# Second-half transposes six steps later, two gate blocks moved ahead of a projection, and mLSTM loads issued one chunk earlier

## The chip, the core and the metric

The kernel runs on one core of one Trainium2 chip. The metric is the device time in microseconds (us) of one execution. Engines are named as the profile names them: PE is TensorE (PEld its weight load), DVE is VectorE, ACT is ScalarE, POOL is GpSimd, and SP is the queue that issues all DMAs of this kernel.

## What is computed

A trunk of two layers for 1024 tokens of width 1024, in float32. Each layer adds a normed mixer and then a normed SwiGLU to the residual stream.

```
for layer in range(2):
    h = rmsnorm(x, pre_mix_g[layer])
    h = ab_mixer(h, ...) if layer == 0 else mlstm_mixer(h, ...)
    x = x + rmsnorm(h, post_mix_g[layer])
    h = swiglu(rmsnorm(x, pre_ffn_g[layer]), w_gate, w_up, w_down)   # width 2816
    x = x + rmsnorm(h, post_ffn_g[layer])

def mlstm_mixer(xn, ...):
    q, k, v, o, ig, fg = split(xn @ w_in + b_in)
    # per chunk of tokens, 8 heads: scores = (q k^T) * exp(decays); num = scores v + inter * (q C)
    # C = decay * C + (w k)^T v          (the state that passes from chunk to chunk)
    h = rmsnorm_per_head(num / max(|den|, exp(-m))) * head_g
    return (sigmoid(o) * h) @ w_out
```

## The kernel before, in words

The 1024 tokens are worked in two halves of 512 (a and b, or A and B in names), each held with features on the partitions. Every float32 operand of a large product is split into a rounded high part and the low rest ("hi", "lo"), and `mm3` makes a product of three matmuls (lines 125 to 127): hi·hi, hi·lo, lo·hi. The high part is a cast on ACT and the low part a subtraction on DVE: lines 106 and 107 for weights streamed by `W`, lines 130 and 131 (`split`) for everything else.

**Order.** The program is written as one main line of matmul blocks. Beside it run "side" generators (norms, transposes, mLSTM); each `yield` of a main block with cost c lets a side advance c times its pace steps. The framework's scheduler then settles the order on each engine, so the order that the engines really hold is shown below where it matters. Each engine works through its own order strictly, and so does the SP queue.

**Feedforward.** Each layer's SwiGLU is done on 2x2 blocks with seven products in place of eight (a Strassen-like scheme): operands are sums and differences of the two token halves and of weight blocks.
- `sandwich` adds the normed mixer output to the residual, norms the result (`xn`), and hands it to a `feature` function. For half B that is `feature_b`: it transposes xn on PE (line 376, into `pt`), evicts on ACT (line 378, `xb` and `xk`), then makes sums and differences on DVE (lines 381, 382, 383, 387) and the splits `s2` and `s3`. `feature_c` later splits `s1`, `a22` and `s4` (twelve operands).
- Meanwhile the main line runs `phase0(LATE)` (PE tile `p`) and `down_first` (PE tile `d`: eleven row blocks m0 to m10 of 12 matmuls, each with an operand from `prep2`: names `r20a`, `whid0a`, `wlod0a` in layer 0, `r21a`, `whid1a`, `wlod1a` in layer 1). When they are done, `down_first` copies its four results on ACT (line 593, `y`).
- Then `phase1` begins. `prep1` loads gate and up weights (`ri`, `rj`), makes four differences for each on POOL (lines 444 to 447: `t14`, `t23`) and splits them (`whit2..g`, `wlot2..g`, then `whit2..u`, `wlot2..u`). The first product `pa` for the gate needs `whit2..g`, the second, for the up weights, needs `whit2..u`.

**mLSTM.** `in1` is the input projection of a half: 24 steps for v and gates (`pv`), 8 blocks for q and k (`pimq`), 8 for the output gate o (`pimo`, sigmoid at line 929). `mlstm` runs a half in four chunks of 128 tokens: loads (`ab`, `iwb`, `qk`, `vt`, each from DRAM), transposes `pc` and `pk`, scores `sc` (line 1018), `pn` (lines 1034, 1036), state update `pu` and `cst` (lines 1045, 1048), the squares of h on ACT (line 1055), a power on POOL (line 1063), the scaling `nu` on DVE (line 1065), and the transposes `ph` (line 1075) that make `yT`. The projection (`popA`, `popB`) multiplies `yT` with `w_out`.

The first half's mLSTM runs beside the second half's `in1`; in the main line it is drained after q and k, and the eight o blocks come behind the projection `popA`, where they cover the norm work of `sandwich` "pA".

Of the kernel before, what the change touches and what calls it, by code (L numbers as in the profile page):

```python
# [8 lines left out]
F32 = mybir.dt.float32  # L9
# [5 lines left out]
P = 128  # L15
# [3 lines left out]
NT = 4  # L19
# [21 lines left out]
def trunk(ctx: ExitStack, tc: tile.TileContext, x, w_in, w_out, w_gate, w_up, w_down,  # L41
          m_in, m_v, m_g, m_out, lru_w, vecs, post_mix, post_ffn, v_bias, out):
    nc = tc.nc
# [10 lines left out]
    def unit(shape, dt=F32, name="u"):  # L54
        return up.tile(shape, dt, tag="u", name=name, bufs=NU)
# [7 lines left out]
    def ps_aux(shape, name):  # L63
        return pp.tile(shape, F32, tag="aux", name=name, bufs=4)
# [56 lines left out]
    W = Stream()  # L121
# [12 lines left out]
    def rstat(src, name, vector=False, junk=None):  # L134
        ss = sp.tile([P, 1], F32, tag="ss", name=f"ss{name}", bufs=4)
        if junk is None:
            junk = sp.tile([P, D], BF16, tag="junk", name=f"junk{name}", bufs=1)
        if vector:
            nc.vector.scalar_tensor_tensor(junk, src, 1.0, src, op0=OP.mult, op1=OP.mult,
                                           accum_out=ss)  # L140
        else:
            nc.scalar.activation(junk, src, AF.Square, accum_out=ss)
        v = sp.tile([P, 1], F32, tag="sv", name=f"sv{name}", bufs=4)
        nc.vector.tensor_scalar(v, ss, 1.0 / D, EPS, op0=OP.mult, op1=OP.add)
        r = sp.tile([P, 1], F32, tag="sr", name=f"sr{name}", bufs=4)
        nc.gpsimd.tensor_tensor(r, v, half[:, 0:1], op=OP.pow)
        return r

    def row(src, name):
        t = sp.tile([P, D + 16], F32, tag="row", name=name, bufs=1)  # L150
        n = src.shape[-1]
        nc.sync.dma_start(t[:, 0:n], src.partition_broadcast(P))
        return t[:, 0:n]

    def load_x(src, t, name):
        xt = unit([P, D], F32, name)
        nc.sync.dma_start(xt, src[t * P:(t + 1) * P])
        return xt

    def scaled(xt, name, vector=False):  # L160
        xn = unit([P, D], F32, f"xn{name}")
        r = rstat(xt, name, vector, xn)
        if vector:
            nc.vector.tensor_scalar(xn, xt, r, None, op0=OP.mult)
        else:
            nc.scalar.activation(xn, xt, AF.Copy, scale=r)
        return xn
# [33 lines left out]
    def sandwich(o, src, dst, g_row, h, g_next, feature, wait=0):  # L201

        name = o.name
        gr = row(g_row, f"gr{name}")
        xn = []
        for t in range(NT):
            while o.ready < t:
                yield
            y = o.y[t]
            rows = slice((h * NT + t) * P, (h * NT + t + 1) * P)  # L210
            xt = load_x(src, h * NT + t, f"xr{name}{t}")
            r = rstat(y, f"p{name}{t}", t % 2 == 1)
            nc.vector.tensor_tensor(y, y, gr, op=OP.mult)
            yield
            nc.vector.scalar_tensor_tensor(xt, y, r, xt, op0=OP.mult, op1=OP.add)
            nc.sync.dma_start(dst[rows], xt)
            yield
            xn.append(scaled(xt, f"n{name}{t}"))
            yield
        for _ in range(wait):  # L220
            yield
        yield from feature(xn, g_next, f"n{name}")
# [71 lines left out]
    class Project:  # L294
# [17 lines left out]
        def run(self, before_last=None):  # L312
            self.prep(0)
            for i, c in enumerate(self.chunks):
                last = i == len(self.chunks) - 1
                if last and before_last is not None:
                    before_last()
                self.prep(i)
                yield from accum_out(self.o, self.st, *c, i == 0, last, f"{self.o.name}{c[0]}")
# [549 lines left out]
    d_v = [dp.tile([NT, P, 8, 129], F32, tag=f"dv{h}", name=f"dv{h}") for h in range(2)]  # L869
    d_qk = [dp.tile([8, P, T], F32, tag=f"dqk{h}", name=f"dqk{h}") for h in range(2)]  # L870
# [63 lines left out]
    def mlstm(m):  # L934
        h = m.h
        while m.gates is None:
            yield
        gi, gf = m.gates
# [35 lines left out]
        nc.sync.dma_start(d_w[h], iw)  # L974
        yield
        m.yT = []
        for c in range(NT):
            cs = slice(c * P, (c + 1) * P)
            ab = unit([P, 8, P], F32, f"ab{h}{c}")
# [2 lines left out]
            dw = d_w[h].rearrange("(a s) j -> s a j", s=2)  # L982
            for s in range(2):
                nc.sync.dma_start(iwb[s * 64:(s + 1) * 64], dw[s, :, cs].partition_broadcast(64))
            qk = unit([P, 8, P], F32, f"qk{h}{c}")
            nc.sync.dma_start(qk, d_qk[h][:, :, cs].rearrange("a p j -> p a j"))
            vt = unit([P, 8, 129], F32, f"vt{h}{c}")
            nc.sync.dma_start(vt, d_v[h][c])
            pc = ps_aux([P, 40], f"pc{h}{c}")
            nc.tensor.transpose(pc, ce[:, cs], ident[0:40, 0:40])  # L990
            cem = sp.tile([P, 40], F32, tag="cem", name=f"cem{h}{c}", bufs=2)
# [49 lines left out]
            if not (h == 1 and c == NT - 1):  # L1041
                for i in range(4):
                    pu = ps_aux([P, 2, 129], f"pu{h}{c}{i}")
                    kwp = kw[:, 2 * i:2 * i + 2].rearrange("p a b -> p (a b)")
                    nc.tensor.matmul(pu, kwp, vt[:, 2 * i:2 * i + 2], start=True, stop=True)
                    for s in range(2):
                        rr = slice(s * 64, (s + 1) * 64)
                        nc.vector.scalar_tensor_tensor(cst[rr, i, s], cst[rr, i, s],
                                                       iwb[rr, i, P - 1:P], pu[rr, s],
                                                       op0=OP.mult, op1=OP.add)  # L1050
                    yield
            ss = sp.tile([P, 8], F32, tag="hss", name=f"hss{h}{c}", bufs=2)
            for hd in range(8):
                junk = sp.tile([P, P], BF16, tag="junkh", name=f"jh{h}{c}{hd}", bufs=1)
# [52 lines left out]
    src_ffn(0, LATE)  # L1107
    src_in1()
    src_in1()
    o_part = W.src[-8:]  # L1110
    del W.src[-8:]
    src_proj(m_out, OUT1)
    W.src += o_part
    src_ffn(1, EARLY)
# [3 lines left out]
    x1 = dp.tile([S, D], F32, tag="x1", name="x1")  # L1118
    x2 = dp.tile([S, D], F32, tag="x2", name="x2")
    x3 = dp.tile([S, D], F32, tag="x3", name="x3")  # L1120
# [3 lines left out]
    def start(gen, pace):  # L1124
        s = [gen, pace, 0.0]
        sides.append(s)
        return s
# [15 lines left out]
    def drain(s):  # L1143
        if s in sides:
            sides.remove(s)
            for _ in s[0]:
                pass
# [10 lines left out]
    def gf(l):  # L1158
        return lambda k: ("g_ffn", 8 * l + k)
# [11 lines left out]
    f0, f1 = Ffn(0), Ffn(1)  # L1171
# [5 lines left out]
    gb = in0(mb, xb)  # L1177
# [8 lines left out]
    run(f0.phase0(EARLY))  # L1186
    drain(sb)
    ob = Out("oB")
    gb = start(sandwich(ob, x, x1, post_mix[0:1], 1, gf(0), f0.feature_b), 1.0)
    run(Project(mb.yT, ob, OUT0).run())  # L1190
    run(f0.phase0(LATE))
    run(f0.down_first())
# [6 lines left out]
    gb = start(sandwich(fb, x1, x2, post_ffn[0:1], 1, gm(1), into(xmb), 8), 1.0)  # L1199
# [4 lines left out]
    gb = in1(nb, xmb)  # L1204
    run(gb, 32)
    drain(sa)
    pa = Out("pA")
    ga = start(sandwich(pa, x2, x3, post_mix[1:2], 0, gf(1), f1.feature_a), 1.2)
    run(Project(na.yT, pa, OUT1).run())
# [3 lines left out]
    run(f1.phase0(EARLY))  # L1213
    drain(sb)
    pb = Out("pB")
    gb = start(sandwich(pb, x2, x3, post_mix[1:2], 1, gf(1), f1.feature_b), 1.0)
    run(Project(nb.yT, pb, OUT1).run())
    run(f1.phase0(LATE))
    run(f1.down_first())
# [5 lines left out]
    gb = start(sandwich_last(eb, x3, out, gr, 1), 1.0)  # L1225
# [91 lines left out]
```

## Time and profile before

| what | value |
|---|---|
| median of 3 runs | 2169.37 us (2169.26 to 2172.45) |
| profiled execution, its own time | 2169.25 us |
| span of the profiled execution | 2167.4 us |
| mean granted PE clock | 0.979 of full speed |
| busy: PE, PEld | 2064.0 us (95%), 1678.2 us (77%) |
| busy: DVE, ACT, POOL | 1494.2 us (69%), 931.7 us (43%), 506.9 us (23%) |

The span is the time from the first to the last instruction; 1.85 us of the execution lie around it. PE is busy nearly all the time, so what a change can save or cost is in the short stretches in which PE waits, and in those in which its clock is granted at half speed. All times in rows are counted from the start of the span.

### The profile page before, as it was taken

The page shows a single profiled execution, that of the slowest core. Times are in us where ns is not written, and L with a number is a line of the kernel's source. Part 1 is how long each engine was busy: PE and PEld are TensorE (multiplying, and loading weights), DVE is VectorE, ACT ScalarE, POOL GpSimd, SP SyncE. Part 2 cuts the span into 40 slices and gives each one's busy share as a digit, 9 for nine tenths or more (in the row PEclk, how much of TensorE's full clock was granted, in tenths as well). Part 3 has the DMA queues.
Part 4 walks back from the last instruction along what each step waited for, and adds up shares of the span by engine and source line. Part 5 has one row for each costly group of instructions (what it writes and reads, how often), then busy time and mean ns, then how long its engine had stood idle before and what let it go on. Part 6 is the DMA issues. An engine that isn't in the chain of part 4 may idle for free.

```text
span 2167.4 us, 26100 instructions
## 1 busy us (share of the span) xinstructions
PE 2064.0 (95%) x9200; PEld 1678.2 (77%) x9200; DVE 1494.2 (69%) x2103; ACT 931.7 (43%) x1317; POOL 506.9 (23%) x371
## 2 busy tenths in 40 slices
PE   7998989988999999999999998999988999999998
PEld 6776766766888887787988987778877888888786
DVE  6988689868876676558553764546459877766567
ACT  6754586446222222446253333645545222223453
POOL 2000100013743336501010000100015744436310
PEclk9999999998999999999999999999998999999999
DMA  6232544446544459967473852667455644469966
GB/s 230 88 122 68 190 141 146 136 160 229 165 160 162 162 182 328 380 201 255 131 257 104 243 178 88 230 188 216 153 177 193 218 162 157 158 211 364 329 223 218
DMA packets 202740, 417.39 MB, mean 193 GB/s; under 512 B 19920, under 2 KB 48720, under 8 KB 202608
## 3 DMA queue, kind: packets, MB, share of 16 engines
q1 hardware_dynamic: 202608, 415.72, 56.9%
q8 instruction: 72, 1.18, 0.2%
q14 instruction: 60, 0.49, 0.1%
HBM read 302.82 MB, written 112.82 MB: 192 GB/s over the span
## 4 chain that ended last, share of the span: by engine, by line
PE 45%; issue 4%; DVE 2%; DMA 2%; ACT 1%; POOL 0%; SPq 0%; DVEq 0%; POOLq 0%; ACTq 0%
PE d L126 4%; PE d L127 3%; PE d L125 3%; PE pb L125 2%; PE pb L126 2%; PE pb L127 2%; PE pc L127 2%; PE pc L126 2%; PE pc L125 2%; PE p L127 2%; PE p L125 2%; PE p L126 2%; PE pv L127 1%; PE pv L125 1%; PE pv L126 1%
## 5 line engine op out<-in xcount | busy, mean ns | idle before, releaser
L107 DVE TENSOR_TENSOR wlo<-raw,whi 128x1024 fp32r<-128x1024 f32 (+2 forms) x164 | 191.5, 1169 | 156.0 <-ACT whi L106 144.9
L106 ACT CAST whi<-raw 128x1024 fp32r<-128x1024 f32 (+2 forms) x164 | 164.6, 1007 | 276.8 <-PE p L126 56.4
L746 DVE SCALAR_TENSOR_TENSOR acc<-cy,vec,acc 128x512 f32<-128x512 f32 x240 | 168.8, 743 | 0.2
L131 DVE TENSOR_TENSOR wlod1s<-r21s,whid1s 128x1024 fp32r<-128x1024 f32 x44 | 56.3, 1286 | 47.7 <-ACT whid1s L130 46.9
L131 DVE TENSOR_TENSOR wlod0s<-r20s,whid0s 128x1024 fp32r<-128x1024 f32 x44 | 57.7, 1314 | 42.2 <-ACT whid0s L130 39.9
L125 PE MATMUL p<-xTnoA,whi 128*128 128x512 f32 x176 | 72.8, 416 | 12.9 <-ACT gel L721 9.1
L130 ACT CAST whid1s<-r21s 128x1024 fp32r<-128x1024 f32 x44 | 46.4, 1054 | 65.2 <-PE d L127 49.4
L130 ACT CAST whid0s<-r20s 128x1024 fp32r<-128x1024 f32 x44 | 46.4, 1054 | 60.5 <-PE d L127 55.5
L126 PE MATMUL p<-xTnoA,whi 128*128 128x512 f32 x176 | 71.9, 408 | 0.0
L1063 POOL TENSOR_TENSOR hrr<-hss,half 128x8 f32<-128x8 f32 x8 | 13.1, 1641 | 251.0 <-DVE hss L1061 251.0
L125 PE MATMUL p<-xTnpA,whi 128*128 128x512 f32 x176 | 71.4, 409 | 0.0
L127 PE MATMUL p<-xTnpA,wlo 128*128 128x512 f32 x176 | 71.1, 404 | 0.0
L126 PE MATMUL p<-xTnpA,whi 128*128 128x512 f32 x176 | 71.0, 403 | 0.0
L126 PE MATMUL d<-wlod0s,whid0s 128*128 128x512 f32 x176 | 69.3, 394 | 1.7 <-DVE wlod0s L131 1.7
L127 PE MATMUL p<-xTnoA,wlo 128*128 128x512 f32 x176 | 70.5, 405 | 0.0
L126 PE MATMUL d<-wlod1s,whid1s 128*128 128x512 f32 x176 | 69.5, 395 | 0.0
L127 PE MATMUL d<-whid1s,wlod1s 128*128 128x512 f32 x176 | 69.4, 394 | 0.0
L127 PE MATMUL d<-whid0s,wlod0s 128*128 128x512 f32 x176 | 68.6, 390 | 0.0
L125 PE MATMUL d<-whid1s 128*128 128x512 f32 x176 | 63.6, 397 | 3.4 <-DVE yeA L611 3.4
L131 DVE TENSOR_TENSOR wlod0a<-r20a,whid0a 128x1024 fp32r<-128x1024 f32 x33 | 44.8, 1363 | 29.4 <-ACT whid0a L130 25.9
L490 DVE TENSOR_TENSOR u<-pc,u 128x512 f32<-128x512 f32 x44 | 30.2, 690 | 44.7 <-PE pc L127 44.7
L540 POOL TENSOR_TENSOR wt<-wq 128x512 f32<-128x512 f32 x22 | 37.2, 1690 | 92.4 <-DMA wq<-in_w_down 52.0
(2481 smaller groups left out, 6561.0 us busy)
## 6 DMA issues: line engine op xcount, KB each, us to landing
wq<-in_w_down SPq DMA_DIRECT2D x88, 256.0 KB, 5.1
ft<-wt SPq DMA_DIRECT2D x88, 256.0 KB, 5.2
raw<-in_w_in SPq DMA_DIRECT2D x32, 512.0 KB, 3.6
raw<-in_m_in SPq DMA_DIRECT2D x32, 512.0 KB, 4.3
raw<-in_w_gate SPq DMA_DIRECT2D x22, 512.0 KB, 4.3
raw<-in_w_up SPq DMA_DIRECT2D x22, 512.0 KB, 3.6
fp<-p1f SPq DMA_DIRECT2D x44, 256.0 KB, 2.1
fs<-s SPq DMA_DIRECT2D x44, 256.0 KB, 3.7
```

The source lines that it names most:

```text
L106: nc.scalar.copy(hi[:, 0:n], raw[:, 0:n])
L107: nc.vector.tensor_tensor(lo[:, 0:n], raw[:, 0:n], hi[:, 0:n].bitcast(F32), op=OP.subtract)
L125: nc.tensor.matmul(ps, l[0], r[0], start=first, stop=False, **kw)
L126: nc.tensor.matmul(ps, l[0], r[1], start=False, stop=False, **kw)
L127: nc.tensor.matmul(ps, l[1], r[0], start=False, stop=last, **kw)
L130: nc.scalar.copy(dst_hi, src)
L131: nc.vector.tensor_tensor(dst_lo, src, dst_hi.bitcast(F32), op=OP.subtract)
L490: TT(u3[k], c[k], u3[k], op=OP.add)
L540: sub(t[0][:, 0], q[0][:, 1], q[0][:, 0], op=OP.subtract)
L746: nc.vector.scalar_tensor_tensor(dst, src[:, k:k + T], V(wname, w0 + k), dst, op0=OP.mult, op1=OP.add)
L1063: nc.gpsimd.tensor_tensor(rr, ss, half, op=OP.pow)
```

## The change

Four edits. Both `sandwich` calls that end in `feature_b` get `wait=6`: six empty steps between the last norm and the first transposition. Two of the eight o blocks of half B are run between the drain of the first mLSTM and the projection `popA`; the weight stream is put in that order. In `mlstm`, `qk` and `vt` of a chunk are issued by a function `load`: those of chunk 0 before the chunk loop, those of chunk c+1 after chunk c's state update.

```diff
+        def load(c):
+            qk = unit([P, 8, P], F32, f"qk{h}{c}")
+            nc.sync.dma_start(qk, d_qk[h][:, :, c * P:(c + 1) * P].rearrange("a p j -> p a j"))
+            vt = unit([P, 8, 129], F32, f"vt{h}{c}")
+            nc.sync.dma_start(vt, d_v[h][c])
+            return qk, vt
+
+        loaded = load(0)
         for c in range(NT):
...
-            qk = unit([P, 8, P], F32, f"qk{h}{c}")
-            nc.sync.dma_start(qk, d_qk[h][:, :, cs].rearrange("a p j -> p a j"))
-            vt = unit([P, 8, 129], F32, f"vt{h}{c}")
-            nc.sync.dma_start(vt, d_v[h][c])
+            qk, vt = loaded
...
+            if c + 1 < NT:
+                loaded = load(c + 1)
             ss = sp.tile([P, 8], F32, tag="hss", name=f"hss{h}{c}", bufs=2)
...
-    o_part = W.src[-8:]
-    del W.src[-8:]
+    o_part = W.src[-6:]
+    del W.src[-6:]
     src_proj(m_out, OUT1)
     W.src += o_part
...
-    gb = start(sandwich(ob, x, x1, post_mix[0:1], 1, gf(0), f0.feature_b), 1.0)
+    gb = start(sandwich(ob, x, x1, post_mix[0:1], 1, gf(0), f0.feature_b, 6), 1.0)
...
     run(gb, 32)
     drain(sa)
+    run(gb, 2)
     pa = Out("pA")
...
-    gb = start(sandwich(pb, x2, x3, post_mix[1:2], 1, gf(1), f1.feature_b), 1.0)
+    gb = start(sandwich(pb, x2, x3, post_mix[1:2], 1, gf(1), f1.feature_b, 6), 1.0)
```

What the scheduler makes of it is seen in the orders. The first place is on PE, layer 0, where `feature_b`'s transposes stand among `down_first`'s matmuls. `xnnoB_3477`, `_3511`, `_3545` and `_3593` are the four normed token tiles in turn; `whid0a_3736` is the first row block's operand. Before:

```order
L127 MATMUL d_3729<-whid0a_3736,wlod0a_3737 128x512
L126 MATMUL d_3730<-wlod0a_3737,whid0a_3736 128x512
L127 MATMUL d_3730<-whid0a_3736,wlod0a_3737 128x512
L376 MATMUL ptnoB_3605<-ident,xnnoB_3545 128x128
L376 MATMUL ptnoB_3612<-ident,xnnoB_3545 128x128
L376 MATMUL ptnoB_3649<-ident,xnnoB_3545 128x128
L376 MATMUL ptnoB_3656<-ident,xnnoB_3545 128x128
L376 MATMUL ptnoB_3605<-ident,xnnoB_3593 128x128
```

The same place on PE in the changed kernel, where `whid0a_3680` and `whid0a_3727` are the first two row blocks' operands:

```order
L125 MATMUL d_3675<-whid0a_3727 128x512
L125 MATMUL d_3676<-whid0a_3680 128x512
L126 MATMUL d_3676<-wlod0a_3681,whid0a_3680 128x512
L127 MATMUL d_3676<-whid0a_3680,wlod0a_3681 128x512
L125 MATMUL d_3676<-whid0a_3727 128x512
L376 MATMUL ptnoB_3635<-ident,xnnoB_3545 128x128
L376 MATMUL ptnoB_3642<-ident,xnnoB_3545 128x128
L376 MATMUL ptnoB_3700<-ident,xnnoB_3545 128x128
L376 MATMUL ptnoB_3707<-ident,xnnoB_3545 128x128
L126 MATMUL d_3673<-wlod0a_3728,whid0a_3727 128x512
```

Before, the third tile's transposes followed 6 `d` matmuls and the fourth's came directly behind them, ahead of the last 12 `p` matmuls. Now those 12 and 16 `d` matmuls stand ahead of the third tile's, and 40 `d` matmuls in all ahead of the fourth's.

The second place is on DVE, layer 1, at the start of `feature_b`'s sums. Before:

```order
L215 SCALAR_TENSOR_TENSOR xrpB_12755<-ypB_12408,srppB_12762,xrpB_12755 128x1024
L144 TENSOR_SCALAR svnpB_12786<-ssnpB_12784 128x1
L381 TENSOR_TENSOR xsnpB_12824<-xbnpB_12792,xknpB_12791 128x512
L382 TENSOR_TENSOR xbnpB_12792<-xanpB_12793,xbnpB_12792 128x512
L383 TENSOR_TENSOR xanpB_12793<-xsnpB_12824,xanpB_12793 128x512
```

And the same place on DVE in the changed kernel:

```order
L215 SCALAR_TENSOR_TENSOR xrpB_12755<-ypB_12408,srppB_12762,xrpB_12755 128x1024
L144 TENSOR_SCALAR svnpB_12786<-ssnpB_12784 128x1
L131 TENSOR_TENSOR wlod1a_13031<-r21a_13027,whid1a_13030 128x1024
L131 TENSOR_TENSOR wlod1a_13050<-r21a_13046,whid1a_13049 128x1024
L131 TENSOR_TENSOR wlod1a_13069<-r21a_13065,whid1a_13068 128x1024
L131 TENSOR_TENSOR wlod1a_13088<-r21a_13084,whid1a_13087 128x1024
L381 TENSOR_TENSOR xsnpB_12852<-xbnpB_12822,xknpB_12821 128x512
```

Four low halves of row blocks m4 to m7 have come ahead of the first sum (m3's and the product at line 423 too, a few rows further up); in layer 0 it is those of m1 to m4 and that product.

The third place is on PE at the end of the first mLSTM, with its last state updates `pu`, the transposes `ph` and the projection `popA`. Before:

```order
L1036 MATMUL pn_10290<-vt_10196,pr_10267 128x129 x2
L1045 MATMUL pu_10296<-vt_10196,kw_10255 128x258
L1045 MATMUL pu_10300<-vt_10196,kw_10255 128x258
L1045 MATMUL pu_10304<-vt_10196,kw_10255 128x258
L1045 MATMUL pu_10308<-vt_10196,kw_10255 128x258
L1075 MATMUL ph_10339<-ident,nu_10270 128x128 x4
L1075 MATMUL ph_10348<-ident,nu_10270 128x128 x4
L125 MATMUL popA_10385<-whi_10137,yspA_10357 128x512
```

The same place on PE in the changed kernel:

```order
L125 MATMUL pimo_10397<-xTnfB_8402,whi_10209 128x512
L126 MATMUL pimo_10397<-xTnfB_8402,whi_10209 128x512
L127 MATMUL pimo_10397<-xTnfB_8402,wlo_10210 128x512
L1083 MATMUL ph_10339<-ident,nu_10270 128x128 x4
L1083 MATMUL ph_10348<-ident,nu_10270 128x128 x4
L125 MATMUL popA_10453<-whi_10359,yspA_10425 128x512
```

The 48 matmuls of two o blocks now stand between the scores and `ph`: 17 of them among the `pn`, 17 between the last `pn` and the last `pu`, and 14 directly ahead of `ph`.

## Rows read from the trace of the kernel before

**Rows 1.** PE's waits, grouped: engine, line, waited for; us in total, times, longest.

```profile
PE ph L1075 <- DVE nu L1065: 6.0, 1, 6.0
...
PE pa L125 <- ACT whit210u L130: 5.2, 1, 5.2
PE pa L125 <- ACT whit200u L130: 5.1, 1, 5.1
PE ptnpB L376 <- ACT xnnpB L166: 4.8, 2, 2.9
PE ptnoB L376 <- ACT xnnoB L166: 4.4, 2, 2.7
...
PE pk L996 <- DMA qk<-dqk: 2.9, 2, 1.9
```

**Rows 2.** Stretches: busy us (instructions) of PE, PEld, DVE, ACT, POOL; granted clock; DMA.

```profile
484.20:494.40 10.20, 5.61 (x20) 3.91 (x19) 3.64 (x8) 6.26 (x9) 1.61 (x3) 0.51 0.72 255
492.66:542.30 49.64, 42.71 (x176) 33.94 (x175) 44.98 (x52) 29.96 (x45) 18.15 (x10) 0.91 0.70 228
1617.50:1627.70 10.20, 6.80 (x21) 5.23 (x22) 4.72 (x8) 6.73 (x12) 0.55 (x1) 0.51 0.75 255
1624.17:1671.04 46.87, 40.82 (x164) 32.28 (x163) 45.98 (x51) 30.28 (x46) 18.67 (x10) 0.86 0.66 219
1306.90:1313.70 6.80, 3.69 (x12) 3.03 (x13) 4.04 (x11) 2.18 (x4) 1.46 (x1) 0.51 0.00 1
```

**Rows 3.** PE in order of time, layer 0: start, us, instruction, [idle before].

```profile
470.39 0.40 PE L125 MATMUL p<-xTnoA,whi 128*128 128x512 f32 x1
470.63 0.39 PE L126 MATMUL p<-xTnoA,whi 128*128 128x512 f32 x1
...
480.25 0.73 PE L125 MATMUL d<-whid0a 128*128 128x512 f32 x2 [0.47 <-ACT whid0a L130]
483.52 0.50 PE L126 MATMUL d<-wlod0a,whid0a 128*128 128x512 f32 x1 [2.53 <-DVE wlod0a L131]
...
490.36 2.37 PE L376 MATMUL ptnoB<-ident,xnnoB 128*128 128x128 f32 x8 [2.72 <-ACT xnnoB L166]
```

**Rows 4.** DVE in order of time, the same columns, both layers' second halves.

```profile
492.66 0.69 DVE L381 TENSOR_TENSOR xsnoB<-xbnoB,xknoB 128x512 f32<-128x512 f32 x1 [4.16 <-ACT xknoB L378]
...
541.09 1.21 DVE L131 TENSOR_TENSOR wlot200u<-t2300u,whit200u 128x1024 fp32r<-128x1024 f32 x1
...
1647.40 1.78 DVE L383 TENSOR_TENSOR xanpB<-xsnpB,xanpB 128x512 f32<-128x512 f32 x1
```

**Rows 5.** POOL and ACT in order of time, layer 0 ahead of the first `pa`.

```profile
519.09 1.30 POOL L444 TENSOR_TENSOR t1400g<-rj00g,ri00g 128x512 f32<-128x512 f32 x1 [29.96 <-DMA rj00g<-in_w_gate]
...
526.89 0.58 ACT L593 COPY y<-d 128x512 f32<-128x512 f32 x1
```

**Rows 6.** DVE groups of 492.66 to 518.50 by form: count, busy us, mean ns, idle before.

```profile
L131 DVE TENSOR_TENSOR wlod0a<-r20a,whid0a 128x1024 fp32r<-128x1024 f32 x8 | 9.8, 1220 | 0.2 <-ACT whid0a L130 0.2
```

**Rows 7.** PE in order of time, layer 1's second half.

```profile
1601.30 0.39 PE L125 MATMUL p<-xTnpA,whi 128*128 128x512 f32 x1
...
1621.88 2.37 PE L376 MATMUL ptnpB<-ident,xnnpB 128*128 128x128 f32 x8 [2.94 <-ACT xnnpB L166]
```

**Rows 8.** PE, DVE and ACT in order of time, from the end of the first mLSTM on.

```profile
1298.15 1.14 PE L1034 MATMUL pn<-cst,qi 128*128 128x258 f32 x4
...
1301.84 1.91 PE L1045 MATMUL pu<-vt,kw 128*128 128x258 f32 x8
1309.77 1.94 PE L1075 MATMUL ph<-ident,nu 128*128 128x128 f32 x8 [6.02 <-DVE nu L1065]
...
1312.97 2.49 DVE L131 TENSOR_TENSOR yspA<-myT,yspA 128x512 fp32r<-128x512 f32 x4
...
1422.37 1.28 ACT L421 ACT_TABLE_LOAD   x1
```

**Rows 9.** DVE in order of time, the first mLSTM's first chunk.

```profile
1200.06 2.19 DVE L999 SCALAR_TENSOR_TENSOR ab<-ab,cem,mask 128x128 f32<-128x128 f32 x8 [4.84 <-DMA ab<-da]
```

## The prediction

> **What bounds the kernel.** I read the page's busy shares first: PE is busy in 95% of the span, so elsewhere than in PE's waits and its half-clock stretches nothing can be gained. Then the grouped waits of PE [rows 1]. The edits aim at three of their kinds: the transposes of half B that wait for the normed tiles (4.4 and 4.8 us), the one wait of 6.0 us at the end of the first mLSTM, and two waits of 2.9 us together for q and k loads. Then the stretches [rows 2], to see what the clock adds: behind each cluster of waits PE runs at 0.51 of full speed, that is mostly at the 1.2 GHz level. It is busy for 5.61 us of such a stretch in layer 0, 6.80 us in layer 1, 3.69 us at the mLSTM's end. Half of that busy time is what the lower level costs: 2.8, 3.4 and 1.8 us. The Trainium skill ("TensorE: Matmul & The Clock Gate", section Terms) prices such time at its length times one minus the granted share, which would be 5.1, 5.1 and 3.4 us; the rows show PE idle for much of it, so I keep the smaller prices.
>
> **Term 1, layer 0's transposes.** At stake are the waits at `ptnoB` of 4.4 us [rows 1], the wait of 2.53 us for the first low half [rows 3] and 2.8 us of clock: 9.7 us. The new order puts 12 `p` and 40 `d` matmuls ahead of the fourth tile's transposes. From 480.25 less 0.47 us, at 0.23 us from start to start [rows 3], those 52 end at 491.8, with the transposes between at about 492.4; the fourth tile was there by 490.36, so those waits go.
>
> What is late next is VectorE. Its first sum of `feature_b` began at 492.66, and from there to the end of `wlot200u`, 542.30 [rows 4], it was busy for 44.98 of 49.64 us [rows 2]. PE's second `pa` product needs that operand. Now the sums begin some 2 us behind those transposes (the evictions of line 378 lie between), at 494.5: 1.8 us later than before. What has moved ahead of them are four low halves of 1.22 us [rows 6] and one product like the sums, 0.69 [rows 4], 5.6 us. So `wlot200u` ends at 542.3 + 1.8 - 5.6 = 538.5, 3.8 us earlier, or up to 4.7 us earlier still if VectorE's idle time (49.64 - 44.98) closes. Against this stands GpSimd: beside its subtractions a VectorE sum takes 1.78 us [rows 4] where it takes 0.69 otherwise (1647.40 against 492.66). `prep1`'s loads follow the low halves through the five `raw` buffers, so the subtractions come earlier too, and into the sums. And ScalarE now has the four copies of line 593, 0.58 us each [rows 5], and the last casts of `s2` and `s3`, shaped alike, ahead of `whit200g`: some 3.4 us, which start only as `d` ends. I take 3 us of gain, bounds +1 (the ScalarE chain decides) to -8.5.
>
> A page states why this can eat the whole gain: by the Trainium skill ("SBUF — State Buffer", section "Who interferes with whom") a VectorE instruction with two SBUF inputs and a GpSimd instruction that reads SBUF exclude each other for a whole instruction. The trace agrees: 0.69 and 1.30 us [rows 4, 5] one after the other are near the 1.78 measured. By that rule eight subtractions of 1.30 us cost VectorE 10.4 us wherever they fall among its sums, and only VectorE's idle time can hide them.
>
> **Term 2, layer 1's transposes.** The same edit, but at stake are 4.8 us of waits and 3.4 of clock. PE now passes 48 `p` and 52 `d` matmuls from 1601.30 before the fourth tile's transposes: 23 us, and with the other transposes about 1626, where they stood at 1621.88 [rows 7]. VectorE's first sum moves from 1624.17 to 1628.2, 4.0 us later; five low halves and the product, 6.8 us, move ahead of it. From there to 1671.04, the end of `wlot210u`, VectorE was busy for 45.98 of 46.87 us [rows 2]: no slack here. So `wlot210u` ends 2.8 us earlier by VectorE's work. But the row blocks m4 to m7 are split early, so the weight loads and GpSimd's subtractions come earlier against the sums, `d` ends long before `whit210g` can be made, and PE's idle time lies in one piece in front of `pa` in place of several. ScalarE reaches `whit210u` only behind `whit210g`, two casts of b22 and twelve of `s1`, `a22` and `s4`, as before. I take 1 us of gain, bounds +3 (half clock longer) to -8.2.
>
> **Term 3, two o blocks ahead of the projection.** From the first `pn` at 1298.15 PE has 5.6 us of work with small gaps, then waits 6.02 us for `nu` [rows 8]. Now 48 matmuls of 0.23 us, 11.1 us, stand in the same stretch, so `ph` starts at 1298.15 + 5.6 + 11.1 = 1314.9. Before, `ph` started at 1309.77 and the 48 came later: 1320.9 by the same count. That is the wait, 6.0 us, and with 1.8 us of clock 7.8. What is late next: `yspA`'s low halves come 3.2 us after `ph` starts [rows 8], and at full clock PE reaches them some 1 us too early (an estimate: the 1.94 us of `ph` shrink by half). Is the chain to `nu` still hidden? Seventeen matmuls (3.9 us) now stand among the `pn`, whose own work is 3.7 us (1298.15 to 1301.84), so the last `pn` ends at 1305.8; `ph` came 7.9 us after that point before, which gives 1313.7. In ScalarE's new order a table load (1.28 us, [rows 8]) and a sigmoid stand ahead of the last two squares: some 2 us, up to 1315.7, so 0.8 us too late. I take 7 us of gain (7.8 less most of that), bounds -4 (the chain stays in sight) to -9. The cover that is gone: behind `popA` six o blocks are left in place of eight, but the order on PE keeps the transposes of `sandwich` pA at the same distance from `popA`, and the gates' chain of the second mLSTM waits for a `p` eviction, not for o blocks. If that cover was needed, up to 11.1 us come back.
>
> **Term 4, q, k and v a chunk ahead.** The two waits for q and k, 2.9 us, go [rows 1]: the loads now stand on SP's queue ahead of `ab`'s and `iwb`'s, and PE's order pulls `pk` and `sc` forward. But in the first chunk VectorE waits until 1200.06 for `ab`, 4.84 us [rows 9], and the `pn` need what follows from it; that load is no earlier in the program, only with less traffic beside it. On SP a load that finds no free buffer holds up the weight loads behind it, which are fetched two to three blocks ahead. I take 2.4 us, bounds 0 to -2.9.
>
> **Sum.** -3 - 1 - 7 - 2.4 = -13.4 us against the profiled execution's 2169.25: 2155.9, so 2156. That execution and the median, 2169.37, differ by 0.1 us. About 0.2% (4.3 us) is what a measurement of this kernel can tell from no change.
>
> **Rivals.**
> 1. Both halves gain in full: the waits and their clock go and VectorE catches up unseen. Then terms 1 and 2 are -9.7 and -8.2, and the sum gives 2169.25 - 27.3 = 2142. For it: VectorE's 4.66 us of idle time in layer 0. Against it: it has 0.9 us in layer 1.
> 2. Only the gate blocks work, and partly: `ab` replaces `qk` as the first chunk's bound (term 4 is 0), terms 1 and 2 are 0 because the wait only moves in front of `pa`, and the chain to `nu` stays in sight (term 3 is -4 to -7): 2162 to 2165. For it: ScalarE's order in front of `whit210u`, and [rows 9].
> 3. Slower: GpSimd's subtractions meet VectorE's sums a second time. Before, the stretch in front of `pa` held them with the idle time of layer 0; if the next round's nine fall into it as well, at 1.78 - 0.69 = 1.1 us each, `wlot2..u` comes 9.8 us later than worked out, so term 1 is +6.0 and term 2 +7.0, and with terms 3 and 4: 2169.25 + 13.0 - 9.4 = 2172.9. It decides from where terms 1 and 2 cost more than 9.4 us together. Against it: the loads of that round wait for `raw` buffers that are freed only by the first round's splits.
> 4. The moves don't take place: excluded for the order, which shows them; each wait could only reappear.
>
> **Chances.** The forecast 0.55 (its own range 2150 to 2160), rival 1 or a good part of it 0.2, rival 2 0.18, rival 3 0.05, other 0.02. Faster by over 0.2% (below 2164.9) holds for the forecast, rival 1 and most of rival 2: 0.87. Within 0.2%: 0.08, from rival 2's upper end and rival 3's lower. Slower: 0.05. The range from 2145 to 2164 leaves out the far end of rival 1 and the slow cases, about 2 in 10.
>
> **What would show it.** Term 1: `ptnoB`'s waits gone, `wlot200u` 2 to 5 us earlier against the start of `p` in this stage (470.39), the half-clock stretch at 484 gone but one in front of or behind `pa` kept. Term 2: a single PE wait of 5 to 11 us in front of `pa` in layer 1, and VectorE sums of 1.7 us earlier than at 1647. Term 3: no wait at `ph`, full clock there, `popA` directly behind with a wait under 2 us. Term 4: no wait for `qk`; perhaps one of VectorE's in its place. The forecast is wrong if the `pa` waits shrink with the transposes' (then rival 1), or if the wait in front of `pa` exceeds what the transposes gave (towards rival 3).

## The result, and the profile after

The changed kernel takes 2158.0 us (median of 5 runs, 2156.3 to 2160.7) against 2169.4; the ratio is 0.9949 with a 95% interval of 0.9935 to 0.9964, so 7.8 to 14.1 us are saved. 2156 was forecast, within 2145 to 2164. The profiled execution took 2157.19 us, its span is 2155.4 us and its mean PE clock 0.986, where it was 0.979.

First the grouped waits of PE in the changed kernel, with the columns of [rows 1]:

```profile
PE pa L125 <- ACT whit210g L130: 9.2, 1, 9.2
...
PE pa L127 <- DVE wlot200u L131: 4.8, 1, 4.8
PE pa L125 <- ACT whit200g L130: 4.3, 1, 4.3
...
PE pa L125 <- ACT whit210u L130: 2.3, 1, 2.3
PE pn L1040 <- DVE qi L1015: 2.2, 1, 2.2
PE pn L1042 <- DVE pr L1032: 2.0, 2, 1.3
PE pa L127 <- DVE wlot200g L131: 1.9, 1, 1.9
...
PE ph L1083 <- DVE nu L1073: 1.0, 1, 1.0
```

Of [rows 1], `ptnoB`, `ptnpB` and `pk` are gone, and `ph` is down from 6.0 to 1.0 us. In their place `pa` waits longer, 22.5 us in these five groups where it waited 10.3, and `pn`, which did not wait, waits 4.2. So of 18.1 us of waits that the edits aimed at, 17.1 left their places and 16.4 came back one step later in the program (smaller groups left aside). What was gained is in good part clock: over the three stretches of the table below PE is busy at half clock for 33.3 us before and 19.8 after, and half of the difference, 6.8 us, is an estimate of what that is worth. These are stretches of the changed kernel, with the columns of [rows 2]:

```profile
519.50:526.30 6.80, 4.19 (x9) 2.91 (x10) 6.80 (x9) 6.80 (x13) 2.02 (x2) 0.51 0.56 205
536.50:539.90 3.40, 2.64 (x6) 2.15 (x7) 3.40 (x4) 1.57 (x2) 3.40 (x2) 0.54 0.00 0
1306.90:1313.70 6.80, 5.12 (x26) 3.87 (x25) 5.13 (x15) 3.03 (x7) 1.64 (x1) 1.00 0.48 155
1642.40:1652.60 10.20, 5.81 (x12) 3.64 (x12) 9.44 (x15) 9.34 (x18) 0.47 (x1) 0.51 0.78 276
1656.10:1659.50 3.40, 3.40 (x10) 2.67 (x9) 3.40 (x3) 0.72 (x1) 3.40 (x3) 0.53 0.10 41
```

The end of the first mLSTM, at 0.51 before [rows 2], is at full clock now, and the two stretches of 10.2 us behind the transposes' waits [rows 2] have no counterpart. What half clock is left in the two feedforward stretches, 10.2 and 13.6 us, lies around `pa`.

Next VectorE of the changed kernel in order of time. The row at 534.92 is layer 0's, the one at 1426.64 is the second mLSTM's, the others are layer 1's sums:

```profile
534.92 2.28 DVE L131 TENSOR_TENSOR wlot200u<-t2300u,whit200u 128x1024 fp32r<-128x1024 f32 x1
...
1426.64 2.19 DVE L1005 SCALAR_TENSOR_TENSOR ab<-ab,cem,mask 128x128 f32<-128x128 f32 x8 [7.77 <-DMA ab<-da]
...
1625.27 0.68 DVE L382 TENSOR_TENSOR xbnpB<-xanpB,xbnpB 128x512 f32<-128x512 f32 x1
1625.99 1.67 DVE L383 TENSOR_TENSOR xanpB<-xsnpB,xanpB 128x512 f32<-128x512 f32 x1
1627.58 2.32 DVE L131 TENSOR_TENSOR wlod1a<-r21a,whid1a 128x1024 fp32r<-128x1024 f32 x1
...
1638.43 1.63 DVE L383 TENSOR_TENSOR xanpB<-xsnpB,xanpB 128x512 f32<-128x512 f32 x1
1640.10 0.69 DVE L387 TENSOR_TENSOR xknpB<-xknpB,xanpB 128x512 f32<-128x512 f32 x1
```

And GpSimd of the changed kernel, where the first and the second round of its subtractions start in either layer, and where layer 1's first round ends:

```profile
504.92 1.38 POOL L444 TENSOR_TENSOR t1400g<-rj00g,ri00g 128x512 f32<-128x512 f32 x1 [18.27 <-DMA rj00g<-in_w_gate]
...
527.53 2.94 POOL L444 TENSOR_TENSOR t1401g<-rj01g,ri01g 128x512 f32<-128x512 f32 x1 [5.93 <-DVE xa22noB L131]
...
1625.55 1.56 POOL L444 TENSOR_TENSOR t1410g<-rj10g,ri10g 128x512 f32<-128x512 f32 x1 [13.61 <-DMA rj10g<-in_w_gate]
...
1637.93 1.59 POOL L447 TENSOR_TENSOR t1410u<-ri10u,t2310u 128x512 f32<-128x512 f32 x1
1652.13 2.37 POOL L444 TENSOR_TENSOR t1411g<-rj11g,ri11g 128x512 f32<-128x512 f32 x1 [12.62 <-DVE xs1npB L131]
```

In layer 0 they began at 519.09 before [rows 5]; in layer 1 GpSimd's row of the kernel before is this:

```profile
1646.49 2.15 POOL L444 TENSOR_TENSOR t1410g<-rj10g,ri10g 128x512 f32<-128x512 f32 x1 [25.85 <-DMA rj10g<-in_w_gate]
```

So they come 14.2 and 20.9 us earlier, since their weights arrive earlier; 2.6 and 8.8 us of this are the earlier start of the stretches as a whole (below), so the move brings some 12 us in either layer. In layer 1 the subtractions now lie on VectorE's eight instructions from 1625.99 to 1640.06, which take 14.1 us where 0.69 each and 1.22 for the low half, the durations on either side, would make 6.1. The difference, 8 us, is of the size of PE's wait in front of `pa`. That it is VectorE's sums that are late there, and not GpSimd's own chain, GpSimd's and ScalarE's rows show: `t2310g`, from which ScalarE casts `whit210g`, is done at 1631.04, but the cast stands behind that of `xs2npB`, which waits for the last of the eight:

```profile
1628.77 2.27 POOL L445 TENSOR_TENSOR t2310g<-rj10g,t1410g 128x512 f32<-128x512 f32 x1
1640.10 0.62 ACT L130 CAST xs2npB<-xanpB 128x512 fp32r<-128x512 f32 x1 [10.10 <-DVE xanpB L383]
```

In layer 1 GpSimd's round lay beside VectorE before as well (1647.40 [rows 4] is one such sum), on the last two sums and the splits behind them; now it lies earlier, ahead of the cast that `pa` waits for.

The start times of rows give the length of the stretches that the edits touch, in each profile: **layer 0** from the first late `p` to the third round's first `pa`; **layer 1** from the first `popB` to the same place there; **mLSTM** from the last q, k matmul of the second half to the first `popB`, which holds the gate blocks and the second mLSTM. Ratios are to runs of the kernel before on the same chip; the times come from several chips, so rows are compared by their ratios, and gains in us are ratios times 2169.4 us.

| kernel | time, us | ratio | 95% interval | layer 0 | layer 1 | mLSTM |
|---|---|---|---|---|---|---|
| before | 2169.4 | 1 | | 119.2 | 170.5 | 254.9 |
| after | 2158.0 | 0.9949 | 0.9935 to 0.9964 | 117.3 | 168.0 | 250.4 |
| transposes' move alone | 2165.2 | 0.9974 | 0.9963 to 0.9984 | 118.3 | 167.9 | 256.9 |
| gate blocks alone | 2162.7 | 0.9973 | 0.9960 to 0.9986 | 119.3 | 172.3 | 248.9 |
| loads ahead alone | 2170.5 | 1.0004 | 0.9993 to 1.0016 | 119.1 | 171.4 | 257.6 |
| after, loads as before | 2160.0 | 0.9954 | 0.9941 to 0.9966 | 117.4 | 169.4 | 249.0 |
| after, no first subtractions | 2135.1 | 0.9846 | 0.9829 to 0.9863 | 106.6 | 153.2 | 250.9 |
| the same, no move | 2161.1 | 0.9964 | 0.9953 to 0.9976 | 118.7 | 166.8 | 249.1 |
| after, eight on VectorE | 2152.8 | 0.9932 | 0.9916 to 0.9948 | 111.4 | 162.6 | 250.2 |
| after, six on VectorE | 2148.0 | 0.9901 | 0.9884 to 0.9917 | 113.4 | 162.0 | 251.3 |
| the same, no move | 2162.5 | 0.9961 | 0.9947 to 0.9976 | 117.1 | 171.3 | 251.3 |
| after, four blocks | 2155.2 | 0.9943 | 0.9928 to 0.9958 | 117.4 | 167.7 | 249.3 |
| six on VectorE, four blocks | 2149.0 | 0.9905 | 0.9888 to 0.9921 | 113.3 | 163.2 | 249.9 |
| after, chunk 0 loaded early | 2157.1 | 0.9958 | 0.9943 to 0.9973 | 117.5 | 168.0 | 255.2 |

### The profile page after: what moved, and what is told of

Its sections match the earlier page's. It is cut to its first block, busy times and chain, and to the rows that moved or that the text cites. A ratio compares the mean times of both kernels' runs of the same rounds, so it can differ in the third digit from the quotient of the medians.

```text
span 2155.4 us, 26100 instructions
## 1 busy us (share of the span) xinstructions
PE 2054.6 (95%) x9200; PEld 1670.9 (78%) x9200; DVE 1508.2 (70%) x2103; ACT 931.4 (43%) x1317; POOL 501.5 (23%) x371
## 4 chain that ended last, share of the span: by engine, by line
PE 44%; issue 4%; DVE 4%; DMA 1%; ACT 1%; POOL 0%; SPq 0%; DVEq 0%; POOLq 0%; ACTq 0%
PE d L126 3%; PE d L127 3%; PE d L125 3%; PE pc L127 2%; PE pc L125 2%; PE pc L126 2%; PE pb L125 2%; PE pb L127 2%; PE pb L126 2%; PE p L125 2%; PE p L126 2%; PE p L127 2%; PE pimq L125 1%; PE pimq L126 1%; PE pimq L127 1%
## 5 line engine op out<-in xcount | busy, mean ns | idle before, releaser
L1071 POOL TENSOR_TENSOR hrr<-hss,half 128x8 f32<-128x8 f32 x8 | 14.2, 1773 | 245.1 <-DVE hss L1069 203.7
L126 PE MATMUL p<-xTnoA,whi 128*128 128x512 f32 x176 | 70.7, 401 | 0.0
L126 PE MATMUL d<-wlod0a,whid0a 128*128 128x512 f32 x132 | 53.6, 406 | 5.2 <-DVE wlod0a L131 5.2
```

The costliest lines, as they stand in the source:

```text
L126: nc.tensor.matmul(ps, l[0], r[1], start=False, stop=False, **kw)
L1071: nc.gpsimd.tensor_tensor(rr, ss, half, op=OP.pow)
```

## The experiments

**One edit at a time.** Each of the first three makes one edit on the kernel before. First the transposes' move:

```diff
-    gb = start(sandwich(ob, x, x1, post_mix[0:1], 1, gf(0), f0.feature_b), 1.0)
+    gb = start(sandwich(ob, x, x1, post_mix[0:1], 1, gf(0), f0.feature_b, 6), 1.0)
...
-    gb = start(sandwich(pb, x2, x3, post_mix[1:2], 1, gf(1), f1.feature_b), 1.0)
+    gb = start(sandwich(pb, x2, x3, post_mix[1:2], 1, gf(1), f1.feature_b, 6), 1.0)
```

> Only the two edits on the transposes (terms 1 and 2), all else as before. From the two traces: layer 0 gave 1.9 us, layer 1 gave 2.6 us, together 4.5 us, so 2169.4 - 4.5 = 2164.9 (ratio 0.998), with one wait in front of pa in layer 1 of about 9 us and none for ptnoB or ptnpB. Rival (the waits only move, and what the pair of traces showed was clock): 2169 (0.9999). Rival (the prediction's rival 1, all of the waits and their clock come back): 2151.5 (0.992).

5.6 us gained (3.5 to 8.0): the move is worth what the traces had shown, and both rivals lie outside the interval. Next the gate blocks:

```diff
-    o_part = W.src[-8:]
-    del W.src[-8:]
+    o_part = W.src[-6:]
+    del W.src[-6:]
     drain(sa)
+    run(gb, 2)
```

> Only the two o blocks ahead of the projection (term 3). The traces show 5.5 us of gain at that place, the prediction said 7: 2169.4 - 5.5 = 2163.9 (ratio 0.9975), by the prediction 2162.4 (0.9968). Rival (the chain to nu stays in sight): 2165.4 or more (0.998). The wait at ph falls from 6 to about 1 us, and there is no stretch at half clock there.

5.9 us gained (3.0 to 8.7), and `ph` waits 1.0 us. The interval holds the prediction's 7, the 5.5 of the pair of traces and the rival's 4; that the chain to `nu` is no longer in sight but for that 1.0 us, PE's grouped waits of this kernel show:

```profile
PE ph L1075 <- DVE nu L1065: 1.0, 1, 1.0
PE popA L127 <- DVE yspA L131: 0.8, 1, 0.8
PE popA L125 <- ACT yspA L130: 0.7, 1, 0.7
```

Then the loads, `load` being the function of the change:

```diff
+        loaded = load(0)
         for c in range(NT):
...
-            qk = unit([P, 8, P], F32, f"qk{h}{c}")
-            nc.sync.dma_start(qk, d_qk[h][:, :, cs].rearrange("a p j -> p a j"))
-            vt = unit([P, 8, 129], F32, f"vt{h}{c}")
-            nc.sync.dma_start(vt, d_v[h][c])
+            qk, vt = loaded
...
+            if c + 1 < NT:
+                loaded = load(c + 1)
```

> Only q, k and v a chunk ahead (term 4). The traces show each mLSTM about 1.0 us longer, with pn waiting for pr and qi in place of pk for qk: 2169.4 + 2.1 = 2171.5 (ratio 1.001). The prediction's term says 2167.0 (0.9989). Rival (it does nothing but move the wait): 2169.4 (1.000).

The counterpart is the changed kernel without this edit:

> The changed kernel without the loads ahead: the transposes' edits and the two o blocks. If the loads cost 2.1 us, this is 2158.0 - 2.1 = 2155.9 (ratio to the kernel before 0.9938). If the prediction's term 4 holds (they gain 2.4 us), it is 2160.4 (0.9959). Rival (the loads change nothing): 2158.0 (0.9949).

Alone the loads change the time by +0.9 us (-1.5 to +3.5); the changed kernel without them can't be told from the one with them, since the intervals overlap nearly whole. The gain of 2.4 us lies outside the first interval, though not the second; the loss of 2.1 us that I had read from one pair of traces lies inside the first, so it is neither confirmed nor excluded. The rival, nothing, is nearest to both runs. All traces agree on the waits: where the loads stand as before (the kernel before, the move alone, the gate blocks alone and this counterpart), `pk` waits 2.9, 4.7, 4.2 and 3.1 us for q and k and `pn` not at all; where they go ahead, `pk` does not wait and `pn` does, 4.2 us in the changed kernel. Loads alone, second mLSTM, PE in order of time:

```profile
1435.48 1.05 PE L1040 MATMUL pn<-cst,qi 128*128 128x258 f32 x2 [2.60 <-DVE qi L1015]
```

**What holds `pa`.** GpSimd's first round of subtractions is left out in both layers; the operands are the weights as loaded, so the output is another.

```diff
+                if m == 0:
+                    t23 = rj.rearrange("p (a t) -> p a t", a=2)
+                    t14 = ri.rearrange("p (a t) -> p a t", a=2)
+                else:
+                    t23 = unit([P, 2, T], F32, f"t23{name}")
+                    t14 = unit([P, 2, T], F32, f"t14{name}")
+                    sub(t14[:, 0], rj[:, 0:T], ri[:, 0:T], op=OP.subtract)
...
```

> The changed kernel without GpSimd's eight subtractions in the first round of gate and up weights in each layer; the two pairs of operands are the weights as they were loaded, so the output differs. Theory (the wait went to pa because VectorE's sums run beside those subtractions at 1.65 to 1.78 us in place of 0.69): in layer 1 VectorE's nine instructions from 1625.99 to 1640.06 take about 6 us in place of 14, so the wait of 9.2 us in front of pa falls to 1 to 3 us and the stretch from popB to pc gets 6 to 8 us shorter; in layer 0 the 12.1 us of waits around pa fall by 5 to 9 us. In all 12 to 17 us: 2141 to 2146 (ratio to the kernel before 0.987 to 0.989). Rival (ScalarE's order, with the y copies and the casts of s2, s3, s1, a22 and s4, is the bound): the pa waits fall by under 2 us a layer, 2154 to 2158.

2135.1 us: by the ratios 22 less than the changed kernel, more than expected. The rival of ScalarE's order is out: `pa` has a single wait left, 0.2 us, with all of ScalarE's copies and casts still to be done. The scheduler also reorders here, since operands are ready earlier, so this measures the subtractions together with what waits for them. VectorE at the place where it took 1.65 to 1.78 us:

```profile
1619.94 0.69 DVE L131 TENSOR_TENSOR xs2npB<-xanpB,xs2npB 128x512 fp32r<-128x512 f32 x1
1620.54 0.68 DVE L131 TENSOR_TENSOR xs3npB<-xbnpB,xs3npB 128x512 fp32r<-128x512 f32 x1
1621.15 0.68 DVE L381 TENSOR_TENSOR xsnpB<-xbnpB,xknpB 128x512 f32<-128x512 f32 x1
1621.75 1.22 DVE L131 TENSOR_TENSOR wlot210g<-rj10g,whit210g 128x1024 fp32r<-128x1024 f32 x1
```

The same work can be kept and put elsewhere:

```diff
-            sub = nc.gpsimd.tensor_tensor
+            sub = (nc.vector if m == 0 else nc.gpsimd).tensor_tensor
```

> The changed kernel with those eight subtractions put on VectorE in each layer's first round, the same result as the reference's. By the theory of mutual exclusion each costs VectorE 0.69 us of its own in place of some 1.0 us lost beside GpSimd, and GpSimd's chain of 1.7 us steps becomes one of 0.7: 8 x 0.69 = 5.5 us against 8 to 8.5 us lost now, so a gain of 2 to 3 us a layer, 2152 to 2154 (ratio 0.992 to 0.993). Rival (the two engines share VectorE's time only in part, and GpSimd's work is mostly free): each layer loses up to 5.5 us, 2163 to 2169 (0.997 to 1.000).

2152.8 us, as the theory of exclusion had it, and the rival is out: VectorE does the eight subtractions itself and is done earlier than with GpSimd doing them beside it (its `wlot200u` ends 63.7 us behind layer 0's first late `p`, in the changed kernel 69.5). Layer 0's stretch is 5.9 us shorter, layer 1's 5.3, more than the time as a whole: one `wlod0s` came ahead of `yfA` in VectorE's order, and PE paid for it in layer 0's second phase, at half clock behind it:

```profile
907.42 0.60 PE L125 MATMUL d<-whid0s 128*128 128x512 f32 x1 [3.52 <-DVE yfA L611]
```

Six of the eight leave that order alone:

```diff
-                sub(t14[:, 1], ri[:, T:], t23[:, 0], op=OP.subtract)
+                nc.gpsimd.tensor_tensor(t14[:, 1], ri[:, T:], t23[:, 0], op=OP.subtract)
```

> As the kernel with the eight subtractions on VectorE, but the fourth of each matrix (the one for t4, needed last) stays on GpSimd, six go. With eight, both feedforward stretches got 5 to 6 us shorter, but the order on VectorE changed at one far place of layer 0's second phase, where one wlod0s came ahead of four sums yfA, and PE waited 3.5 us for yfA and fell to half clock. With six that order is as in the changed kernel. Theory (the gain of eight was there and was given back at yfA): the stretch from the second round of phase 1 to the second layer's mLSTM is back at 620 to 622 us in place of 626.7, and the time is 2147 to 2150 (ratio 0.990 to 0.991). Rival (the 6 us lost there were chance, clock and all): 2152 to 2154 like the eight.

2148.0 us, as expected; the stretch from layer 0's second round to the second layer's mLSTM is back at 621.9 us. It beats both kernels. Its VectorE rows show sums and subtractions at one price, and its groups of PE's waits hold 16.8 us for `pa`, where the changed kernel has 22.5 in the five groups above alone:

```profile
1635.97 0.69 DVE L387 TENSOR_TENSOR xknpB<-xknpB,xanpB 128x512 f32<-128x512 f32 x1
1636.58 0.69 DVE L444 TENSOR_TENSOR t1410g<-rj10g,ri10g 128x512 f32<-128x512 f32 x1
```

```profile
PE pa L127 <- DVE wlot200u L131: 4.0, 1, 4.0
PE pa L125 <- ACT whit210g L130: 3.8, 1, 3.8
...
PE pa L125 <- ACT whit200g L130: 3.4, 1, 3.4
...
PE pa L127 <- DVE wlot200g L131: 2.4, 1, 2.4
...
PE pa L125 <- ACT whit210u L130: 2.0, 1, 2.0
...
PE pa L127 <- DVE wlot210g L131: 0.6, 1, 0.6
PE pa L125 <- ACT whit200u L130: 0.6, 1, 0.6
```

**Did the collision eat the move's gain?** Both kernels again with the transposes where they were, first the one without the subtractions.

```diff
-    gb = start(sandwich(ob, x, x1, post_mix[0:1], 1, gf(0), f0.feature_b, 6), 1.0)
+    gb = start(sandwich(ob, x, x1, post_mix[0:1], 1, gf(0), f0.feature_b), 1.0)
...
-    gb = start(sandwich(pb, x2, x3, post_mix[1:2], 1, gf(1), f1.feature_b, 6), 1.0)
+    gb = start(sandwich(pb, x2, x3, post_mix[1:2], 1, gf(1), f1.feature_b), 1.0)
```

> As the kernel without the first round's subtractions (the output differs in the same way), but with the transposes where they stood before, both wait=6 taken out. Theory (VectorE's collision with GpSimd is what ate the transposes' gain, so without it the move is worth most of what was at stake, 9.7 and 8.2 us): 8 to 16 us slower than with the move, 2143 to 2151 (ratio 0.988 to 0.992). Rival (the move is worth its 4.8 us whatever GpSimd does, and the subtractions cost the kernel before as much): 2140 (0.987).

2161.1 us, 26 more than with the move: beyond what either theory said, and not clean, because the order on ScalarE changed too: its copies `y` stand behind twelve casts, and PE waits for one of them.

```profile
528.67 0.80 PE L125 MATMUL pa<-xs2noB,whit200g 128*128 128x512 f32 x1 [7.06 <-ACT y L597]
```

The same with six subtractions on VectorE, where the `y` copies stand nearly as in the kernel before:

> Six subtractions of the first round on VectorE, as in the kernel of 2148 us, but with the transposes where they stood before (both wait=6 taken out). The kernel without the subtractions and without the move had come out 26 us slower than the one with the move, but there ScalarE's order had also put its y copies behind twelve casts (PE waited 7.1 us for one) and one wlod0s ahead of yfA, so its size says little; here that order is as in the kernel before. Theory (the collision had eaten part of the transposes' gain, so the move is worth more once the collision is eased): 8 to 12 us slower than with the move, 2156 to 2160 (ratio 0.9935 to 0.995). Rival (the move is worth its 4.8 us in any case): 2153 (0.992). Second rival (the six alone give nothing without the move, as in the pair without subtractions): 2162 to 2164 (0.997), the time of the gate blocks and loads alone.

2162.5 us, the second rival: without the move the six give some 3.5 us over gate blocks and loads (0.9973 times 1.0004 is 0.9977, against 0.9961), which is within the intervals; with it they give 10.4 (0.9949 to 0.9901). So the move is worth 4.8 us beside GpSimd's subtractions (stretches: 1.6 in layer 0 and 3.2 in layer 1, means of five profiles with it and three without) and 13 us between the two kernels with six of them on VectorE (0.9961 to 0.9901; stretches 3.7 and 9.3). Not all of the 13 us is the collision's. This is the kernel without the move; VectorE first, when the weights arrive in layer 0:

```profile
515.84 0.69 DVE L444 TENSOR_TENSOR t1400g<-rj00g,ri00g 128x512 f32<-128x512 f32 x1 [0.71 <-DMA rj00g<-in_w_gate]
...
522.42 0.69 DVE L444 TENSOR_TENSOR t1400u<-rj00u,ri00u 128x512 f32<-128x512 f32 x1 [1.32 <-DMA rj00u<-in_w_up]
```

There the sums are over when the weights come, so no collision with them is left to ease. What PE waits for is ScalarE: `whit200u` stands in its order behind casts and copies that follow each other without a gap, as in the kernel before (5.1 us [rows 1]). Layer 1 has a wait of its own. PE's waits, then the chain behind the second of them, from the SP queue, GpSimd and VectorE:

```profile
PE pa L125 <- ACT whit200u L130: 4.8, 1, 4.8
...
PE pa L127 <- DVE wlot210u L131: 3.5, 1, 3.5
```

```profile
SPq L439 <- POOL t1410g L447: 14.6, 1, 14.6
```

```profile
1642.39 10.56 POOL L447 TENSOR_TENSOR t1410g<-ri10g,t2310g 128x512 f32<-128x512 f32 x1 [31.45 <-DVE t2310g L445]
```

```profile
1657.23 0.69 DVE L477 TENSOR_TENSOR u210g<-pa,u210g 128x512 f32<-128x512 f32 x1 [5.40 <-DMA u210g<-fp]
```

The load of `rj11g` waits for the subtraction that was left on GpSimd, which takes 10.56 us here; the load of `u210g` stands behind it on the queue; VectorE stands idle for that load, and PE gets `wlot210u` late. With the move, `u210g`'s load stands ahead of `rj11g`'s, and VectorE does not wait for it. So up to 3.5 of the 13 us are the queue's order. That the collision ate part of the move's gain is what the runs with the move show (at least 22.5 us of waits at `pa` against 16.8); how much of the difference between 4.8 and 13 us it is stays open.

**Two smaller questions.** Four o blocks in place of two, alone and with the six:

```diff
-    o_part = W.src[-6:]
-    del W.src[-6:]
+    o_part = W.src[-4:]
+    del W.src[-4:]
-    run(gb, 2)
+    run(gb, 4)
```

> The changed kernel with four o blocks between the first mLSTM and its projection in place of two (the scheduler puts 65 of their matmuls ahead of ph, 48 before). Theory (the chain to nu was still 1.0 us in sight, and yspA's halves cost another 2.1 us in front of popA): ph's wait goes, popA's waits stay in part, 1 to 2 us gained at that place, 2156 to 2157. Rival (the cover behind popA gives out, as it leaves four blocks in place of six): the transposes of the first half's feedforward wait, and 1 to 8 us come back, 2159 to 2166.

> Six subtractions on VectorE and four o blocks ahead of the projection, on top of the changed kernel. If the two add up (8 to 10 us from the one, 1 to 2.5 from the other): 2145 to 2148 (ratio 0.989 to 0.990). Rival (four blocks were worth nothing, their better time was chance): the same as with six subtractions alone.

`ph` and `popA` have no wait left, the mLSTM stretch is 1.1 and 1.4 us shorter, and the times can't be told from those with two blocks. The rival, that cover behind `popA` gives out, is not seen.

Chunk 0's q, k and v at the start of each mLSTM:

```diff
         gi, gf = m.gates
...
+        loaded = load(0)
...
-        loaded = load(0)
         for c in range(NT):
```

> The changed kernel with chunk 0's q, k and v loaded at the start of each mLSTM, ahead of its gate chain, in place of directly ahead of ab's loads. Theory (qk and vt ahead of ab on the queue delay ab, on which VectorE waits 7.8 us in the second mLSTM where it waited 6.4): that wait falls by 1 to 1.5 us, pn's wait for qi of 2.2 us falls by as much, 2155.5 to 2157. Rival (the time to ab is that of its own store and load, whatever else is on the queue): no change, 2158.

No change that can be measured; the profile is that of the slowest of its eight executions (2163.7 us), so its mLSTM stretch of 255.2 us, with 10.2 us more of half clock than the changed kernel's, says little. In it `pn` still waits 2.9 us for `qi`, and VectorE 7.1 us for `ab`. That q, k and v delay `ab` on the queue is not supported.

## Why the prediction held, step by step

**Term 1** (-3): the mechanism was right, the size less: 1.6 us. `wlot200u` begins 70.7 us behind the first `p` before [rows 3, 4] and 67.2 after (534.92, with `p` at 467.75), 3.5 us earlier, but it takes 2.28 us where it took 1.21 [rows 4], so its end comes 2.5 us earlier, where 3.8 had been worked out. PE waits 4.8 us for it all the same, since it reaches `pa` earlier too.

**Term 2** (-1): 3.2 us. The single wait of 9.2 us in front of `pa` came as described, and the sums of 1.7 us begin at 1625.99, where one stood at 1647.40 [rows 4]. The way to the gain was another than the term's: `wlot210u` ends only some 0.4 us earlier within its stretch, where 2.8 had been worked out. The prediction named the collision of GpSimd's subtractions with the sums but gave it no price in this term; it took VectorE as full by its own work, and the experiments show that 8 of its 14 us there are GpSimd's.

In PE's account the move's waits went and came back, and the clock was gained. Over the stretches (the same means of five profiles with the move and three without) PE is idle for 14.6 us with it and 14.2 without in layer 0, 12.6 and 13.2 in layer 1, while its busy time at half clock falls from 12.3 to 8.0 and from 12.8 to 8.7 us. Half of these differences, 2.2 and 2.1 us, is an estimate of the clock's part. One of the prediction's own signs of being wrong came with it: `pa`'s waits grew by 12.2 us in the groups above, more than the 9.2 us that the transposes gave, which it had read as a step towards rival 3; the time fell all the same.

Rival 1 (all of it comes back) is what the kernel comes nearer to once the collision is eased: 13 us between the two kernels with six subtractions moved, up to 3.5 of them the queue's, where 17.9 were at stake. Rival 3 (they meet a second time) came true in part: the second rounds start at 527.53 and 1652.13, ahead of the up weights' low halves, and `wlot200u` takes longer for it; it came nowhere near deciding. The rule that the prediction drew from the Trainium skill ("SBUF — State Buffer", section "Who interferes with whom") is borne out in its direction: by the price that it worked out from the rule, eight subtractions cost VectorE 10.4 us beside it, and on it they take eight times 0.69. Beside it the trace has 8 us, and moved onto it they saved time.

**Term 3** (-7): the stretch from the last q, k matmul to the first `p` behind it (layer 1's) is 114.5 us in the three profiles without the blocks moved and 108.3 in the nine with two: 6.2 us, with 1.0 us of `ph` still in sight, about the 0.8 that the term had allowed.

**Term 4** (-2.4, bounds 0 to -2.9): this step failed. `ab` replaces `qk` as the bound, as rival 2 had it; pulling `pk` and `sc` ahead only moves the wait behind them to `pn`. The bounds should have reached above nothing. From the first `p` of layer 1 to `popB`, four of the seven profiles with loads ahead (those with four blocks or the early chunk 0 aside) have 3.4 us of half clock, and none of the four without; the means are 142.5 and 141.1 us. In time nothing is left of it.

**The sum.** By stretches -1.6, -3.2, -6.2 and about +1.4 make -9.6, by ratio it is -11.1 (7.8 to 14.1 saved), -13.4 was forecast. That the sum came so near is in part luck: by stretches term 2 gave 2.2 us more than forecast, which makes up for what terms 1 and 3 gave less (1.4 and 0.8), so that the miss is term 4's. The two profiled executions differ by 12.1 us, but 2.6 of them lie ahead of the first changed instruction, and are the clock's.

## What to carry to other kernels

When a wait on the bound engine is removed by moving work behind it, ask which loads move up with it, and on whose instructions the work that they feed will fall: here the weights came some 12 us earlier and GpSimd's use of them landed on VectorE's sums, for which PE waited. On such a stretch an operation is cheaper on the engine that is full (0.69 us) than beside it on an idle one (about 1 us lost), and two edits of which each uncovers the other's bound can be worth more than their sum (16.5 us here, where one gave 4.8 and the other some 3.5; part of the difference is a wait that only the kernel with the second edit alone has). A load brought forward gains only if it is the last to arrive for the work that the bound engine waits for; look for the next operand of the same instruction first.

## What the runs showed of the hardware that I had not expected

The granted clock falls at places where nothing changed. The program is the same up to layer 0's late `p`, yet that part takes from 465.5 to 470.4 us in these profiles, with 20.5 to 30.7 us at half clock in it. Two stretches, first of the kernel before:

```profile
334.10:337.50 3.40, 3.40 (x9) 2.17 (x8) 3.40 (x7) 3.36 (x6) 0.00 (x0) 0.53 0.00 0
419.40:422.80 3.40, 2.59 (x6) 2.11 (x7) 3.16 (x6) 0.00 (x0) 0.00 (x0) 0.53 0.00 0
```

and the same of the changed kernel:

```profile
334.10:337.50 3.40, 1.93 (x9) 1.28 (x8) 3.40 (x7) 3.37 (x5) 0.00 (x0) 1.00 0.00 0
419.40:422.80 3.40, 3.40 (x14) 2.45 (x13) 1.82 (x4) 0.00 (x0) 0.00 (x0) 1.00 0.00 0
```

So two profiles of this kernel can't be compared end to end to better than some 5 us; an edit of 1 to 3 us is to be read from its own stretch, in several profiles.

GpSimd can lose far more beside VectorE than the 1 us that VectorE loses beside it. The subtraction that takes 10.56 us in the row above takes 11.18 us in the kernel with the move and six subtractions on VectorE, and 1.75 us in the changed kernel. In both long cases VectorE's instructions follow each other without a gap for the first 9 us of it. GpSimd's spans are rough in a profile, but the queue's wait of 14.6 us ended with it. Why GpSimd gets its turn sooner in the changed kernel no run here shows.
